# Two more 8-column products in the gate of the mLSTM branch of a hybrid layer

## The chip, the cores and the metric

The kernel runs on one core of a Trainium2 chip. The metric is the time of one execution on the device in microseconds (us), as the median over several executions. Beside it stands one execution that the hardware profiler recorded; times inside the kernel are read from that one and are counted from the start of its span.

## What is computed

One layer with two branches over 256 tokens of width 1024, all in 32-bit floats. The input is normalised and modulated by a condition vector; one wide product with `w_in` gives thirteen pieces; an attention branch and an mLSTM branch are worked out, gated, added, and multiplied by `w_out`:

```python
h = _rmsnorm(x, norm_w) * (1 + scale) + shift
(qa, ka, va, za, qm, km, vm, zm, om, ig, fg, ga, gm) = jnp.split(h @ w_in, SPLIT_IDX, axis=-1)
...
ya = (ya * jax.nn.silu(za)) @ w_att_proj
...
hm = jax.nn.sigmoid(heads(om, ML_HEADS).astype(f32)) * hm
hm = _rmsnorm(hm, ml_norm_w.reshape(ML_HEADS, 1, ML_HEAD_DIM))
ym = (merge(hm).astype(x.dtype) * jax.nn.silu(zm)) @ w_ml_proj
y = jax.nn.sigmoid(ga) * ya + jax.nn.sigmoid(gm) * ym
return x + gate * (y @ w_out)
```

The change sits in the product that gives `gm`, the gate of the mLSTM branch.

## The kernel before

Every large product is made of three products of rounded operands. A weight block is split into a high part `wh` (cast by ACT, line 472) and a low part `wl` (by DVE, line 478), the activations into `hTh` and `hTl`, and the sum high·high + high·low + low·high replaces one product at full precision.

The program is a list of chunks (`za`, `qm`, `zm`, `km`, `att`, `vm`, `ga`, `om`, `gm`, `ml`, `out` and others), each cut into steps of 256 rows of the weight matrix. The order of work is the order in which the Python code emits it, queue by queue; no scheduler moves anything. At each step the code emits the split of the block that is wanted four steps later, then the work hung on that step by `at(step, fn)` (other parts of the layer), then the step's own products.

A step of `gm` is one of the weight-stationary kind: 2 blocks of 128 rows, 4 column blocks `i` for each, and three products of 256 columns for each of these, so 24 products, every one with its own weight load. `gm` has two halves of four steps. They are called steps 1 to 8 below; step 1 starts at 270.58 us, step 2 at 275.56, step 3 at 278.39, step 4 at 282.28, step 5 at 285.11, step 6 at 288.72, step 7 at 292.43 and step 8 at 295.37.

The inner loop of such a step, with line numbers of the profile:

```python
 1205  extra = EXTRA.get((ch["name"], ch["half"], kp, i)) if kk == 0 else None
 1206  if extra == 0:
 1207      nc.tensor.matmul(aux([128, 8]), wh[:, 0, cs], sh_[:, k, 0:8], start=True, stop=True)
 1208  nc.tensor.matmul(o, wh[:, kk, cs], sh_[:, k], ...)
 1210  if extra == 1:
 1211      nc.tensor.matmul(aux([128, 8]), wh[:, 0, cs], sh_[:, k, 0:8], start=True, stop=True)
 1212  nc.tensor.matmul(o, wh[:, kk, cs], sl_[:, k], ...)
 1213  nc.tensor.matmul(o, wl[:, kk, cs], sh_[:, k], ...)
```

So a table `EXTRA` places additional products of 8 columns. Their result is never read. The key is chunk, half, step in the half and column block, counted from 0; the value 0 puts the product ahead of the first of the three, the value 1 behind it. The table before holds six of them; the one in `gm` stands in step 7.

Each additional product needs a place to write: `aux(...)` takes one of four PSUM buffers named `aux`, the one that has been released longest. The same four buffers serve the attention, the transposes and `ml_num`, and an instruction that takes a buffer waits until its last readers are done.

`ml_num(h)` is the work that stands between the steps of `gm`. For one head it takes two `aux` buffers, makes 9 products of 256 or 258 columns (lines 914 to 916), and each buffer is then read by DVE (line 918, `omt<-aux`) and by ACT (line 919, `den<-aux`). One head is emitted ahead of step 1, two heads ahead of step 2 (so all four buffers), one ahead of step 4. Ahead of steps 6 and 7 stand 8 transposes each (line 954), also into `aux`.

Of the kernel before, what the change touches and what calls it, by code (L numbers as in the profile page):

```python
# [64 lines left out]
def tile_hybrid(ctx: ExitStack, tc: tile.TileContext, x, c, params, params2, rel_t, w_row, ada_mod, ada_gate,  # L65
# [241 lines left out]

    chunks = []

    EXTRA = {('za', 0, 0, 0): 0, ('qm', 0, 2, 1): 0, ('qm', 0, 2, 2): 1, ('km', 0, 0, 0): 0, ('ga', 0, 0, 0): 0, ('gm', 1, 2, 0): 1}  # L310
    STRASSEN = ('zm', 'vm', 'om')

    def seg(kind, src, c0, name, stat=None):
# [827 lines left out]
    for g in range(NG):  # L1141
# [49 lines left out]
        for kk in range(2):  # L1191
# [9 lines left out]
            else:  # L1201
                for i in range(4):
                    cs = slice(i * 128, (i + 1) * 128)
                    o = mmt[ci][:, i]
                    extra = EXTRA.get((ch["name"], ch["half"], kp, i)) if kk == 0 else None
                    if extra == 0:
# [71 lines left out]
```

## Time and profile before

| | |
|---|---|
| median of 3 executions | 346.86 us (346.7 to 347.53) |
| the profiled execution, whole | 347.67 us |
| its span (first to last instruction) | 345.5 us |
| TensorE matmuls (PE) busy | 339.3 us, 98% of the span, 2324 instructions |
| VectorE (DVE) busy | 297.8 us, 86% |
| ScalarE (ACT) busy | 243.4 us, 70% |
| granted TensorE clock, mean | 0.999 of full |

PE is the matmul side of TensorE and PEld its weight loads, which run beside the matmuls. A busy time counts overlapping instructions once. The recorded length of one matmul (about 0.28 us for 256 columns) is longer than the distance from its start to the next one's start, since matmuls are pipelined; what a product costs is read from the distance of the starts.

### The profile page before, as it was taken

The page shows a single profiled execution, that of the slowest core. Times are in us where ns is not written, and L with a number is a line of the kernel's source. Part 1 is how long each engine was busy: PE and PEld are TensorE (multiplying, and loading weights), DVE is VectorE, ACT ScalarE, POOL GpSimd, SP SyncE. Part 2 cuts the span into 40 slices and gives each one's busy share as a digit, 9 for nine tenths or more (in the row PEclk, how much of TensorE's full clock was granted, in tenths as well). Part 3 has the DMA queues.
Part 4 walks back from the last instruction along what each step waited for, and adds up shares of the span by engine and source line. Part 5 has one row for each costly group of instructions (what it writes and reads, how often), then busy time and mean ns, then how long its engine had stood idle before and what let it go on. Part 6 is the DMA issues. An engine that isn't in the chain of part 4 may idle for free.

```text
span 345.5 us, 6083 instructions
## 1 busy us (share of the span) xinstructions
PE 339.3 (98%) x2324; PEld 315.0 (91%) x2324; DVE 297.8 (86%) x435; ACT 243.4 (70%) x376; POOL 87.8 (25%) x90
## 2 busy tenths in 40 slices
PE   8899999999999999999999999999999999999996
PEld 8778889988999999888999998899988999999885
DVE  5989996887988877999786899998988988989793
ACT  3868779989877756689688557874497758744440
POOL 4960002774100815002353273000000022500000
PEclk9999999999999999999999999999999999999999
DMA  7999999997567499179760973929969379074011
GB/s 274 413 419 417 418 390 336 258 223 308 171 224 288 64 338 282 47 296 371 262 229 2 348 201 65 379 104 335 279 184 416 112 276 409 2 262 166 2 61 61
DMA packets 30116, 83.72 MB, mean 242 GB/s; under 512 B 2176, under 2 KB 6280, under 8 KB 29576
## 3 DMA queue, kind: packets, MB, share of 16 engines
q1 hardware_dynamic: 27520, 78.08, 62.3%
q0 software_dynamic: 2112, 4.19, 7.1%
q10 hardware_dynamic: 456, 1.07, 0.9%
q8 instruction: 18, 0.29, 0.3%
q14 instruction: 10, 0.08, 0.1%
HBM read 81.89 MB, written 1.45 MB: 241 GB/s over the span
## 4 chain that ended last, share of the span: by engine, by line
PE 92%; DMA 7%; DVE 0%; ACTq 0%; issue 0%; DVEq 0%
PE mm L1208 15%; PE mm L1212 15%; PE mm L1213 15%; PE pm L192 7%; DMA adat<-in_ada_mod_dram 6%; PE aux L1187 6%; PE aux L1189 6%; PE aux L1188 6%; PE mm L1198 4%; PE mm L1200 3%; PE mm L1199 3%; PE pg L192 2%; DMA prm<-in_params_dram 1%; PE mm L1226 1%; PE mm L1225 1%; PE mm L1224 1%
## 5 line engine op out<-in xcount | busy, mean ns | idle before, releaser
L478 DVE TENSOR_TENSOR wl<-raw,wh 128x1024 fp32r<-128x1024 f32 (+2 forms) x90 | 107.0, 1214 | 16.6 <-ACT wh L472 16.6
L472 ACT CAST wh<-raw 128x1024 fp32r<-128x1024 f32 (+2 forms) x100 | 100.6, 1024 | 27.3 <-PE mm L1212 19.3
L1208 PE MATMUL mm<-hTh,wh 128*128 128x256 f32 x320 | 89.7, 280 | 0.0
L1212 PE MATMUL mm<-hTl,wh 128*128 128x256 f32 x320 | 88.8, 277 | 0.0
L1213 PE MATMUL mm<-hTh,wl 128*128 128x256 f32 x320 | 88.6, 277 | 0.0
L1213 PEld LDWEIGHTS mm<-hTh,wl 128*128 128x128 f32 x320 | 60.3, 188 | 0.0
L1208 PEld LDWEIGHTS mm<-hTh,wh 128*128 128x128 f32 x320 | 60.1, 188 | 0.1
L1212 PEld LDWEIGHTS mm<-hTl,wh 128*128 128x128 f32 x320 | 60.1, 188 | 0.0
L478 POOL TENSOR_TENSOR wl<-raw,wh 128x1024 fp32r<-128x1024 f32 x10 | 24.4, 2455 | 51.7 <-ACT wh L472 51.7
L1198 PE MATMUL mm<-wh,hTh 128*128 128x512 f32 (+2 forms) x64 | 23.0, 360 | 0.0
L1200 PE MATMUL mm<-wh,hTl 128*128 128x512 f32 (+2 forms) x64 | 22.4, 350 | 0.0
L1199 PE MATMUL mm<-wl,hTh 128*128 128x512 f32 (+2 forms) x64 | 22.4, 350 | 0.0
L181 DVE TENSOR_TENSOR wrl<-raw,wrh 128x512 fp32r<-128x512 f32 (+1 forms) x24 | 19.1, 818 | 0.3
L1187 PE MATMUL aux<-wh,Sh 128*128 128x512 f32 x48 | 18.7, 389 | 0.0
L1188 PE MATMUL aux<-wl,Sh 128*128 128x512 f32 x48 | 18.7, 389 | 0.0
L1189 PE MATMUL aux<-wh,Sl 128*128 128x512 f32 x48 | 18.7, 389 | 0.0
L151 DVE CUSTOM_DVE_ANT_0 sq<-adat,cb 128x1024 f32<-128x1024 f32 x14 | 17.1, 1218 | 1.5 <-DMA adat<-in_ada_mod_dram 1.5
L1208 PE MATMUL mm<-yah,wh 128*128 128x256 f32 x64 | 17.8, 279 | 0.0
L1213 PE MATMUL mm<-yah,wl 128*128 128x256 f32 x64 | 17.7, 276 | 0.0
L1212 PE MATMUL mm<-yal,wh 128*128 128x256 f32 x64 | 17.7, 276 | 0.0
L1213 PE MATMUL mm<-ymh,wl 128*128 128x256 f32 x64 | 17.7, 276 | 0.0
L1208 PE MATMUL mm<-ymh,wh 128*128 128x256 f32 x64 | 17.7, 276 | 0.0
(266 smaller groups left out, 842.8 us busy)
## 6 DMA issues: line engine op xcount, KB each, us to landing
raw<-in_w_in_dram SPq DMA_DIRECT2D x34, 1024.0 KB, 7.4
adat<-in_ada_mod_dram SPq DMA_DIRECT2D x16, 512.0 KB, 9.6
raw<-in_w_row_dram SPq DMA_DIRECT2D x8, 704.0 KB, 9.7
gw<-in_ada_gate_dram SPq DMA_DIRECT2D x4, 1024.0 KB, 8.9
raw<-in_w_att_proj_dram SPq DMA_DIRECT2D x4, 1024.0 KB, 9.9
raw<-in_w_ml_proj_dram SPq DMA_DIRECT2D x4, 1024.0 KB, 6.6
raw<-in_w_out_dram SPq DMA_DIRECT2D x4, 1024.0 KB, 4.9
raw<-in_w_in_dram POOLq DMA_DIRECT2D x3, 1024.0 KB, 13.1
```

Source lines behind the costliest of these rows:

```text
L192: nc.tensor.matmul(pm[ch][:, t], a[:, k, t * 128:(t + 1) * 128], b[:, cs], start=k == 0 and i == 0, stop=k == KT - 1 and i == 2)
L472: nc.scalar.copy(h, w)
L478: e.tensor_tensor(l, w, h.bitcast(F32), op=OP.subtract)
L1187: nc.tensor.matmul(o, a, wh[:, kk], start=k == 0 and p in (0, 1, 3), stop=False, skip_group_check=True)
L1188: nc.tensor.matmul(o, a, wl[:, kk], start=False, stop=False, skip_group_check=True)
L1189: nc.tensor.matmul(o, b, wh[:, kk], start=False, stop=k == 3, skip_group_check=True)
L1198: nc.tensor.matmul(o, a, wh[:, kk], start=first, stop=False)
L1199: nc.tensor.matmul(o, a, wl[:, kk], start=False, stop=False)
L1200: nc.tensor.matmul(o, b, wh[:, kk], start=False, stop=last)
L1208: nc.tensor.matmul(o, wh[:, kk, cs], sh_[:, k], start=first and i % 2 == 0, stop=False, skip_group_check=True)
L1212: nc.tensor.matmul(o, wh[:, kk, cs], sl_[:, k], start=False, stop=False, skip_group_check=True)
L1213: nc.tensor.matmul(o, wl[:, kk, cs], sh_[:, k], start=False, stop=last and i % 2 == 1, skip_group_check=True)
```

## The change

Two entries are added to the table. Nothing else differs in the code.

```diff
-    EXTRA = {('za', 0, 0, 0): 0, ('qm', 0, 2, 1): 0, ('qm', 0, 2, 2): 1, ('km', 0, 0, 0): 0, ('ga', 0, 0, 0): 0, ('gm', 1, 2, 0): 1}
+    EXTRA = {('za', 0, 0, 0): 0, ('qm', 0, 2, 1): 0, ('qm', 0, 2, 2): 1, ('km', 0, 0, 0): 0, ('ga', 0, 0, 0): 0, ('gm', 0, 1, 0): 1, ('gm', 0, 3, 0): 1, ('gm', 1, 2, 0): 1}
```

They put one 8-column product behind the first product of step 2 and one behind the first product of step 4. PE gets two more matmuls with their weight loads; the queues of DVE, ACT, POOL and SP hold the same instructions in the same order as before.

PE at the start of step 2, before. The numbers tell buffers apart: `aux_3086` is the last of the four buffers that the two heads ahead of step 2 have taken, `mm_3006` is the accumulator of `gm`.

```order
L914 MATMUL aux_3086<-vaug_2526,SD_2239 128x258
L915 MATMUL aux_3086<-vml_2527,SD_2239 128x256
L916 MATMUL aux_3086<-vaug_2526,SD_2239 128x258
L1208 MATMUL mm_3006<-hTh_71,wh_2968 128x256
L1212 MATMUL mm_3006<-hTl_72,wh_2968 128x256
L1213 MATMUL mm_3006<-hTh_71,wl_2969 128x256
```

The same place now, with the waits named (a semaphore carries the name of the engine that raises it).

```order
L914 MATMUL aux_3086<-vaug_2526,SD_2239 128x258
L915 MATMUL aux_3086<-vml_2527,SD_2239 128x256
L916 MATMUL aux_3086<-vaug_2526,SD_2239 128x258
L1208 MATMUL mm_3006<-hTh_71,wh_2968 128x256
L1211 MATMUL aux_3101<-hTh_71,wh_2968 128x8 [waits Activation_49]
L1212 MATMUL mm_3006<-hTl_72,wh_2968 128x256
L1213 MATMUL mm_3006<-hTh_71,wl_2969 128x256
```

The new product stands second in step 2 and waits for ACT. Its buffer `aux_3101` is the place in PSUM that `aux_3059` had, the first buffer of the first of the two heads, and the count it waits for is the one that ACT reaches with its read of `aux_3059`.

ACT around that read (the same rows in both programs): `den` is the read at line 919, `sqm` the square at line 921, `wh` a cast of the split.

```order
L919 ACTIVATE den_3007<-aux_3017 128x1 [waits DVE_49]
L921 ACTIVATE sqm_3026,ssq_3008<-omt_2949 128x256
L472 CAST wh_3055<-raw_2686 128x1024 [waits PE_49]
L919 ACTIVATE den_3007<-aux_3059 128x1 [waits DVE_49]
L921 ACTIVATE sqm_3065,ssq_3008<-omt_2949 128x256 [waits Activation_49]
L919 ACTIVATE den_3007<-aux_3067 128x1 [waits DVE_49]
```

The read of `aux_3059` stands behind the cast that belongs to step 2, and itself waits for DVE, whose queue holds the subtraction of that split (line 478) ahead of its own read of `aux_3059` (line 918). Nothing moved in this queue; what is new is that the product of line 1211 on PE is tied to this read.

PE at step 4, now; the product of the head ahead of it has lost its wait for ACT, since it takes the buffer of the first additional product.

```order
L914 MATMUL aux_3169<-vaug_2526,SD_2239 128x258 [waits PE_49]
L915 MATMUL aux_3169<-vml_2527,SD_2239 128x256
L916 MATMUL aux_3169<-vaug_2526,SD_2239 128x258
L914 MATMUL aux_3177<-vaug_2526,SD_2239 128x258 [waits Activation_49]
L915 MATMUL aux_3177<-vml_2527,SD_2239 128x256
L916 MATMUL aux_3177<-vaug_2526,SD_2239 128x258
L914 MATMUL aux_3177<-vaug_2526,SD_2239 128x258
L915 MATMUL aux_3177<-vml_2527,SD_2239 128x256
L916 MATMUL aux_3177<-vaug_2526,SD_2239 128x258
L1208 MATMUL mm_3006<-hTh_71,wh_2990 128x256
L1211 MATMUL aux_3204<-hTh_71,wh_2990 128x8 [waits Activation_49]
L1212 MATMUL mm_3006<-hTl_72,wh_2990 128x256
```

The wait for ACT of line 914 has moved from here to step 2. The second additional product takes the place of `aux_3078`, the first buffer of the second head ahead of step 2, and waits for ACT's read of that.

## The prediction

> **What bounds the kernel now.** I read the head of the page first, then what PE waited for, then the chain.
>
> ```profile
> span 345.5 us, 6083 instructions
> PE 339.3 (98%) x2324; PEld 315.0 (91%) x2324; DVE 297.8 (86%) x435; ACT 243.4 (70%) x376; POOL 87.8 (25%) x90
> PEclk9999999999999999999999999999999999999999
> PE 92%; DMA 7%; DVE 0%; ACTq 0%; issue 0%; DVEq 0%
> ```
>
> PE is busy for 98% of the span, and the chain that ended last lies on PE for 92% of it. The waits of PE, in full:
>
> ```profile
> PE warm L217 <- POOL ident masks.py:199: 1.4, 1, 1.4
> PE pm L192 <- DVE wrl L181: 1.0, 2, 0.6
> PE pm L192 <- ACT hTh L164: 0.5, 1, 0.5
> ```
>
> All three lines (217 and 192) belong to the opening phase. In `gm` and behind it PE waits for nobody, so a delay put into PE there has no slack to vanish in: every later product, and the output behind the last one, moves by it. For the same reason each nanosecond between two products counts. That distance has two values. The windows of two steps of 24 products with nothing else in them, step 3 of `gm` and one of `ga`:
>
> ```profile
> 278.39:281.22 2.83, 2.83 (x27) 2.83 (x25) 2.08 (x4) 2.06 (x9) 0.00 (x0) 1.00 0.91 327
> 231.40:234.12 2.72, 2.72 (x26) 2.72 (x25) 2.72 (x5) 1.06 (x1) 0.00 (x0) 1.00 0.14 15
> ```
>
> The first figure is the length of the step: 2.83 us is 118 ns a product, 2.72 us is 113 ns, both at a granted clock of 1.00. So a stretch of products runs in a wide or in a close spacing; steps 1 to 6 of `gm` run wide, and step 7, where the sixth additional product stands, goes over to close. This is read from the starts in PE's timeline. An additional product that does so in a place like the new ones, behind a first product of a wide stretch, stands in `qm`, and what followed the one in step 7 is below it:
>
> ```profile
> 125.03 0.17 PE L1207 MATMUL aux<-hTh,wh 128*128 128x8 f32 x1
> 125.06 0.36 PE L1208 MATMUL mm<-hTh,wh 128*128 128x256 f32 x1
> 125.26 0.28 PE L1212 MATMUL mm<-hTl,wh 128*128 128x256 f32 x1
> 125.38 0.28 PE L1213 MATMUL mm<-hTh,wl 128*128 128x256 f32 x1
> 125.50 0.28 PE L1208 MATMUL mm<-hTh,wh 128*128 128x256 f32 x1
> 125.62 0.17 PE L1211 MATMUL aux<-hTh,wh 128*128 128x8 f32 x1
> 125.65 0.36 PE L1212 MATMUL mm<-hTl,wh 128*128 128x256 f32 x1
> 125.85 0.28 PE L1213 MATMUL mm<-hTh,wl 128*128 128x256 f32 x1
> ...
> 292.86 0.28 PE L1213 MATMUL mm<-hTh,wl 128*128 128x256 f32 x1
> ...
> 295.37 0.28 PE L1208 MATMUL mm<-hTh,wh 128*128 128x256 f32 x1
> ```
>
> From the first product to the third it takes 0.35 us with the additional one between (125.50 to 125.85). The remaining 22 distances of step 7 take 295.37 − 292.86 = 2.51 us, which is 114 ns each: close after a few products.
>
> **The change part by part.** It removes nothing and moves nothing; it adds two products with their weight loads, and a wait.
>
> *The wait in step 2.* This is the largest term. PE and its weight loads around the place:
>
> ```profile
> 275.56 0.28 PE L1208 MATMUL mm<-hTh,wh 128*128 128x256 f32 x1
> 275.68 0.28 PE L1212 MATMUL mm<-hTl,wh 128*128 128x256 f32 x1
> 275.80 0.28 PE L1213 MATMUL mm<-hTh,wl 128*128 128x256 f32 x1
> ```
>
> ```profile
> 275.57 0.19 PEld L1212 LDWEIGHTS mm<-hTl,wh 128*128 128x128 f32 x1
> ```
>
> The new product's weight load would stand where that load stands, at 275.57. It must first see ACT's read (line 919) of the first buffer of the first head. ACT, then DVE:
>
> ```profile
> 274.91 1.04 ACT L472 CAST wh<-raw 128x1024 fp32r<-128x1024 f32 x1
> 277.57 0.17 ACT L919 ACTIVATE den<-aux 128x1 f32<-128x1 f32 x1 [1.62 <-DVE omt L918]
> ```
>
> ```profile
> 275.98 1.23 DVE L478 TENSOR_TENSOR wl<-raw,wh 128x1024 fp32r<-128x1024 f32 x1 [0.56 <-ACT wh L472]
> 277.12 1.08 DVE L918 TENSOR_TENSOR omt<-aux,omt 128x256 f32<-128x256 f32 x3
> ```
>
> The read ends at 277.57 + 0.17 = 277.74. It is late for a reason that PE can't speed up: ACT casts until 275.95, DVE subtracts until 277.2, then reads the buffer, then ACT does. What a release of PE by ACT costs is seen once in the opening phase:
>
> ```profile
> 10.86 0.60 ACT L164 ACTIVATE hTh<-xnT,Bb,Ab 128x256 fp32r<-128x256 f32 x1 [0.95 <-DVE Bb L144]
> ```
>
> ```profile
> 11.51 0.30 PEld L192 LDWEIGHTS pm<-wrh,hTh 128*128 128x128 f32 x2 [0.67 <-ACT hTh L164]
> ```
>
> ACT ends at 11.46, the load starts at 11.51: 0.05 us. So the load of the new product starts at 277.79 in place of 275.57, **2.22 us** later. Behind it on PE are queued the other 23 products of step 2 and all that follows. ACT and DVE wait for PE (buffers of `wh`) and slide with it, at most as far; their queues ahead of the read hold nothing that needs a product of step 2.
>
> *The new product itself in step 2.* First to third product takes 0.35 us with an additional one and 275.80 − 275.56 = 0.24 us without: **0.11 us**. Its 8 columns are not what it costs, since the next product is recorded only 0.03 us later (125.62 to 125.65) and the one behind that 0.20 later. The Trainium skill ("TensorE: Matmul & The Clock Gate", section "Back-to-back issue gap") has a matmul of 64 columns or fewer start its successor after some 60 cycles, with a floor of about 25 ns; by that the two new products would cost 0.05 us together in place of 0.22 and the sum below would be 0.17 lower. The 0.03 agrees with the floor, the 0.20 behind it does not fit a price of that size, and the measured 0.11 is used.
>
> *The second wait, in step 4.* It is for ACT's read of the third buffer; DVE's three reads above end at 278.20, and ACT's third follows within some 0.5 us as its first did, so it is over by 278.7, and PE comes there after 282.4. Nothing; if ACT were 3 us later, this would be the next wait.
>
> *The spacing behind the new products.* If they do what the one in `qm` did, the wide steps become close ones. The rows of the other steps:
>
> ```profile
> 282.28 0.28 PE L1208 MATMUL mm<-hTh,wh 128*128 128x256 f32 x1
> ...
> 282.51 0.28 PE L1213 MATMUL mm<-hTh,wl 128*128 128x256 f32 x1
> ...
> 285.11 0.28 PE L1208 MATMUL mm<-hTh,wh 128*128 128x256 f32 x1
> ...
> 287.93 1.03 PE L954 MATMUL aux<-ident,omt 128*128 128x128 f32 x8
> 288.72 0.36 PE L1208 MATMUL mm<-hTh,wh 128*128 128x256 f32 x1
> ...
> 291.64 0.60 PE L954 MATMUL aux<-ident,omt 128*128 128x128 f32 x4
> ```
>
> ```profile
> 90.74 0.37 PE L1208 MATMUL mm<-hTh,wh 128*128 128x256 f32 x1
> ...
> 93.56 0.38 PE L743 MATMUL aux<-kT,qT 128*128 128x256 f32 x1
> ```
>
> Step 2, the 22 distances behind its third product: 278.39 − 275.80 = 2.59 against 2.51, −0.08. Step 3: 2.83 against 2.72, −0.11. Step 4: the additional product +0.12 (0.35 against 0.23), the rest 2.60 against 2.51, −0.09; together +0.03. Step 5: 2.82 against 2.72, −0.10. Step 6 comes behind transposes; a step of `za` behind transposes that runs close takes 93.56 − 90.74 = 2.82, step 6 took 2.92: −0.10. Steps 7 and 8 run close already. Whether a close spacing comes about is bounded from both sides: none of it gives 0 for these five terms and leaves the 0.12 of step 4; all of it gives −0.48 in the steps, and up to 0.04 more if the 9 products ahead of step 4 (281.22 to 282.28) go from 118 to 113 ns too. I take the steps and leave out the 0.04, as these nine stood between no two close steps before.
>
> *Sum:* 2.22 + 0.11 − 0.08 − 0.11 + 0.03 − 0.10 − 0.10 = **+1.97 us**. Against the profiled execution that is a span of 345.5 + 1.97 = 347.5 and a whole of 347.67 + 1.97 = 349.6. That execution lies 0.8 us above the median shown; the time asked for is the median, so 346.86 + 1.97 = **348.8 us**, 0.57% longer.
>
> **The rivals.**
>
> *The wait comes, the close spacing doesn't.* The wait breaks the rhythm that the product in `qm` had around it, and shortly ahead of that one another additional product (125.03 above) left the spacing wide (125.26 to 125.38 to 125.50, 0.12 each). Then 2.22 + 0.11 + 0.12 = 2.45: 349.3. For it: no stall ahead of a stretch of 256 columns is in this trace, so the state after one is unknown.
>
> *The sixth additional product upsets what is close already.* It would now find steps 5 and 6 close, and could turn them wide from step 7 on through `ml`. That is about 23 + 24 + 192 = 239 products by 4.5 ns, 1.1 us more: 349.9. Against it: the spacing kept close behind the transposes in `za`.
>
> *PE's clock drops in the wait.* A step at half the granted clock takes 2.72 us more: 351.5 for one such step. Against it: the pause of 0.67 us quoted above and the others of PE's waits, 1.4 us in the longest, left the clock row at 9 throughout; but 2.2 us is longer than any of them. The Trainium skill (same page, "Part 1", on the clock gate) lets the clock fall after an idle window of about 3.4 us, which this wait does not reach; no run here shows it.
>
> *No wait to speak of: not slower.* If ACT's read were done before 275.52 (275.57 less the 0.05), the change would be only what its two products do: 0.11 + 0.12 − 0.48 = −0.25, 346.6, the same within what can be told. This decides at one point: how far behind 275.52 the read ends. The profile has it 2.2 us behind, held by three instructions in a row: the cast of 1.04, the subtraction of 1.23, and DVE's read from 277.12 until ACT can begin at 277.57. To fall below the 0.3% it would have to end 0.9 us earlier.
>
> **How the numbers follow.** A measurement of this kernel can tell about 0.3% from no change, 1.04 us. The forecast gets 0.62, the wait without close spacing 0.20, the upset from step 7 on 0.05, the clock 0.05, and no wait or a much shorter one 0.08. The first three and the clock are slower by over 0.3%: 0.92. Of the last 0.08, 0.06 is within 0.3% and 0.02 faster, which would need more than all the close spacing there is to win. The range runs from 348.2, 0.6 below the forecast (the spread of the three times shown is 0.8, and the 0.04), to 349.9, the third case. Outside it are the clock, the missing wait and some of the spread, under 2 in 10.
>
> **What would show it.** In the profile of the changed kernel PE, or its weight loads, should carry a wait at line 1211 for ACT's `den` of line 919, once, of some 2 us, starting near 275.6, and none for the second of these products. The starts from the product behind it on should lie some 2.3 us later than before. Steps 3 and 5 should take 2.72 us each in place of 2.83 and 2.82; if they take 2.83, the first rival holds. Steps 7 and 8 and `ml` should keep their close spacing. The clock row should stay at 9. The prediction is wrong if ACT's read comes much earlier than 277.7, or if PE does not stand still for it.

## The result, and the profile after

| | before | changed |
|---|---|---|
| median of 5 executions each, same chip | 346.86 us (346.43 to 347.62) | 349.93 us (349.28 to 351.04) |
| ratio, 95% interval | | 1.0087 (1.0072 to 1.0103) |
| the profiled execution, whole / span | 347.67 / 345.5 us | 351.04 / 348.9 us |

The change costs 3.07 us. The forecast was 1.97 us, 348.8: the sign and the cause of the larger part were right, and the time lies at the upper edge of the range (349.9), where the second rival stands.

The head of the page of the changed kernel:

```profile
span 348.9 us, 6087 instructions
PE 340.7 (98%) x2326; PEld 315.9 (91%) x2326; DVE 297.9 (85%) x435; ACT 243.0 (70%) x376; POOL 87.1 (25%) x90
PEclk9999999999999999999999999999999989999999
```

PE's busy time grew by 1.4 us and the span by 3.4, and the clock row has one 8: the 33rd of 40 slices, which begins at 279.1 us (32 × 348.9 / 40), in step 2. What the weight loads waited for (engine, tile and line, releaser, total, count, longest), and the loads around the place:

```profile
PEld aux L1211 <- ACT den L919: 2.2, 1, 2.2
```

```profile
274.83 0.19 PEld L1208 LDWEIGHTS mm<-hTh,wh 128*128 128x128 f32 x1
277.18 0.19 PEld L1211 LDWEIGHTS aux<-hTh,wh 128*128 128x128 f32 x1 [2.16 <-ACT den L919]
277.29 0.19 PEld L1212 LDWEIGHTS mm<-hTl,wh 128*128 128x128 f32 x1
```

ACT and DVE ahead of it, in the changed kernel:

```profile
276.96 0.17 ACT L919 ACTIVATE den<-aux 128x1 f32<-128x1 f32 x1 [1.63 <-DVE omt L918]
```

```profile
275.37 1.23 DVE L478 TENSOR_TENSOR wl<-raw,wh 128x1024 fp32r<-128x1024 f32 x1 [0.56 <-ACT wh L472]
276.51 1.41 DVE L918 TENSOR_TENSOR omt<-aux,omt 128x256 f32<-128x256 f32 x4
```

PE's own rows there, the first product of step 2, the new product, and the third product of the step:

```profile
274.95 0.28 PE L1208 MATMUL mm<-hTh,wh 128*128 128x256 f32 x1
277.18 0.27 PE L1211 MATMUL aux<-hTh,wh 128*128 128x8 f32 x1 [1.96 <-ACT den L919]
...
277.51 0.28 PE L1213 MATMUL mm<-hTh,wl 128*128 128x256 f32 x1
```

The wait is there once, at line 1211, for the read that was named. Step 1 starts at 269.96 here and at 270.58 before, so places are compared from the start of step 1. ACT's read ends 7.17 us behind it (276.96 + 0.17 − 269.96) and ended 7.16 behind it before; the load follows 0.05 us later (277.13 to 277.18); and it stands at 7.22 where the next load stood at 4.99 before: 2.23 us later. From the first to the third product of step 2 it takes 277.51 − 274.95 = 2.56 us against 0.24, so the wait and the new product's own slot are 2.32 together. Those two terms were forecast as 2.33.

Two more losses are not in the forecast sum. The first is in this same execution. PE's windows in the changed kernel (start:end, length, busy times of PE, PEld, DVE, ACT, POOL, granted clock, DMA): step 2 up to a point, the stretch behind it, and one step of `ml`:

```profile
274.95:278.19 3.24, 1.28 (x11) 1.08 (x10) 2.83 (x6) 1.61 (x9) 0.00 (x0) 1.00 0.98 338
278.19:281.61 3.42, 3.42 (x19) 3.42 (x17) 0.93 (x2) 0.70 (x5) 0.00 (x0) 0.50 0.70 271
...
301.44:304.16 2.72, 2.72 (x26) 2.72 (x25) 2.72 (x3) 2.25 (x3) 1.05 (x1) 1.00 0.00 0
```

```profile
277.99 0.28 PE L1208 MATMUL mm<-hTh,wh 128*128 128x256 f32 x1
278.10 0.30 PE L1212 MATMUL mm<-hTl,wh 128*128 128x256 f32 x1
278.21 0.40 PE L1213 MATMUL mm<-hTh,wl 128*128 128x256 f32 x1
278.41 0.42 PE L1208 MATMUL mm<-hTh,wh 128*128 128x256 f32 x1
278.62 0.41 PE L1212 MATMUL mm<-hTl,wh 128*128 128x256 f32 x1
```

A microsecond after PE has started again, the granted clock falls to 0.50 for 3.42 us, and the products stand 0.21 us apart in place of 0.11. Then it is full again. The step of `ml` runs close (2.72), as before.

The second loss shows itself where the clock holds. The changed kernel was run again beside other kernels, and that time the profiled execution (350.02 us, span 347.9) kept its clock. Its windows are, in this order, steps 2, 3, 4, 5, 6, 7, 8 and the first step of `ml`:

```profile
274.65:279.81 5.16, 3.20 (x27) 2.99 (x26) 3.75 (x7) 2.33 (x13) 0.00 (x0) 1.00 0.93 326
279.81:282.64 2.83, 2.83 (x26) 2.83 (x25) 1.59 (x4) 1.05 (x1) 0.00 (x0) 1.00 0.29 117
283.71:286.57 2.86, 2.86 (x28) 2.86 (x26) 2.27 (x6) 1.08 (x7) 1.30 (x2) 1.00 0.97 368
286.57:289.29 2.72, 2.72 (x26) 2.72 (x25) 2.69 (x8) 2.25 (x3) 2.06 (x3) 1.00 1.01 383
290.08:293.00 2.92, 2.92 (x27) 2.92 (x26) 2.92 (x7) 2.15 (x5) 0.00 (x0) 1.00 1.03 435
293.79:296.82 3.03, 3.03 (x29) 3.03 (x27) 1.56 (x4) 3.00 (x5) 1.88 (x1) 1.00 0.14 51
296.82:299.64 2.82, 2.82 (x26) 2.82 (x25) 2.82 (x3) 1.30 (x2) 1.94 (x2) 1.00 0.00 0
299.64:302.47 2.83, 2.83 (x26) 2.83 (x25) 2.83 (x4) 2.25 (x3) 1.05 (x1) 1.00 0.00 0
```

Step 5 is close (2.72), as forecast. Steps 3 and 6 are not. Step 8 and `ml`, which run close before (2.72 each), are wide here: 2.82 and 2.83. So the same program takes its loss in two ways, and which of them an execution shows is not the same each time.

### The profile page after: what moved, and what is told of

Same layout as the page of the kernel before. It is cut to its first block, busy times and chain, and to the rows that moved or that the text cites. A ratio compares the mean times of both kernels' runs of the same rounds, so it can differ in the third digit from the quotient of the medians.

```text
span 348.9 us, 6087 instructions
## 1 busy us (share of the span) xinstructions
PE 340.7 (98%) x2326; PEld 315.9 (91%) x2326; DVE 297.9 (85%) x435; ACT 243.0 (70%) x376; POOL 87.1 (25%) x90
## 5 line engine op out<-in xcount | busy, mean ns | idle before, releaser
L1208 PEld LDWEIGHTS mm<-hTh,wh 128*128 128x128 f32 x320 | 61.0, 191 | 0.1
L1212 PEld LDWEIGHTS mm<-hTl,wh 128*128 128x128 f32 x320 | 60.9, 190 | 0.0
```

The costliest lines, as they stand in the source:

```text
L1208: nc.tensor.matmul(o, wh[:, kk, cs], sh_[:, k], start=first and i % 2 == 0, stop=False, skip_group_check=True)
L1212: nc.tensor.matmul(o, wh[:, kk, cs], sl_[:, k], start=False, stop=False, skip_group_check=True)
```

## The experiments

The theory at the outset: the wait for ACT's read makes the loss, and the spacing of the products moves the rest. Its rivals: that the additional products cost it by themselves, through the spacing they leave behind them (above all by what happens to `ml`), and that the clock does. All kernels compute the whole layer; what is edited is where the additional products stand, where they write, or what stands ahead of the read.

The kernels ran in three groups on three chips, each group beside executions of the kernel before on the same chip: its medians there were 347.19 us (29 executions, for the first four kernels), 346.92 (20, the next four) and 347.00 (21, the last two). From one execution to the next the part ahead of `gm` takes up to a microsecond more or less (step 1 starts between 269.67 and 270.58 us in the twelve profiles), so beside the medians stands one length read from PE's timeline of each profiled execution: from the first product of step 1 of `gm` to the first product of `out` (steps 1 to 8 and all of `ml`). Before it is 319.85 − 270.58 = 49.27 us.

**The wait taken away.** Both new products stay where they are, but write into a buffer of the accumulators (`mm`, two buffers, one of them free through the first half of `gm`) in place of an `aux` buffer. Lines behind it move by one.

```diff
-    nc.tensor.matmul(aux([128, 8]), wh[:, 0, cs], sh_[:, k, 0:8], start=True, stop=True)
+    free8 = ps.tile([128, 8], F32, name="mm", bufs=2) if (ch["name"], ch["half"]) == ("gm", 0) else aux([128, 8])
+    nc.tensor.matmul(free8, wh[:, 0, cs], sh_[:, k, 0:8], start=True, stop=True)
```

> Both new products stay where they are, but write into the free accumulator of the large products in place of a buffer of ml_num, so nothing is waited for. Theory (the wait is what costs, with the drop of the clock that can follow it): no wait of PE in gm, granted clock 1.0 there, time 346.5 to 347.1 us, ratio 0.999 to 1.001. Rival (the products themselves cost, by upsetting the spacing of what follows): slower by 1 us or more, ratio above 1.003, without a wait.

Measured: 347.84 us (11 executions), ratio 1.0021 (1.0011 to 1.003). PE in it, at the new product of step 2 (now line 1212), and two steps of `ml`:

```profile
275.04 0.28 PE L1208 MATMUL mm<-hTh,wh 128*128 128x256 f32 x1
275.16 0.17 PE L1212 MATMUL mm<-hTh,wh 128*128 128x8 f32 x1
275.19 0.36 PE L1213 MATMUL mm<-hTl,wh 128*128 128x256 f32 x1
275.39 0.28 PE L1214 MATMUL mm<-hTh,wl 128*128 128x256 f32 x1
```

```profile
297.62:300.45 2.83, 2.83 (x27) 2.83 (x25) 2.83 (x4) 2.25 (x3) 1.06 (x1) 1.00 0.00 0
300.45:303.28 2.83, 2.83 (x27) 2.83 (x26) 2.83 (x5) 1.34 (x2) 0.00 (x0) 1.00 0.26 65
```

First to third product: 0.35 us, no wait. Most of the loss is gone, so the wait makes most of it; but the time misses the expected 0.999 to 1.001. What is left, about 0.7 us, is there without any wait and with the clock at 1.00: steps 2 to 5 are close and gain, but `ml` is wide. The length from step 1 to `out` is 50.18 us, 0.91 more than before.

**The product of step 2 alone**, with its wait.

```diff
-    ('gm', 0, 1, 0): 1, ('gm', 0, 3, 0): 1, ('gm', 1, 2, 0): 1}
+    ('gm', 0, 1, 0): 1, ('gm', 1, 2, 0): 1}
```

> Only the new product of step 2, with its wait. Theory: all of the loss, ratio 1.006 to 1.010, a wait of 2.2 us of the weight loads at line 1211 for ACT. Rival (each of the two products costs its share): about half, ratio near 1.004.

Measured: 349.81 us (6), ratio 1.0081 (1.0063 to 1.0098); in 2 of the 6 executions the mean clock was 0.995 (350.92 and 350.68 us), in the others it was full (349.01 to 349.90). The profiled execution is one of the latter, with the same wait of 2.2 us. Its windows: steps 2 and 3, then step 4, and a step of `ml`:

```profile
274.78:279.85 5.07, 3.10 (x27) 2.90 (x26) 3.75 (x7) 2.33 (x13) 0.00 (x0) 1.00 0.94 334
279.85:282.57 2.72, 2.72 (x26) 2.72 (x25) 1.48 (x4) 1.05 (x1) 0.00 (x0) 1.00 0.33 128
283.64:286.47 2.83, 2.83 (x26) 2.83 (x25) 2.23 (x5) 1.09 (x7) 1.30 (x2) 1.00 0.88 340
...
299.46:302.18 2.72, 2.72 (x27) 2.72 (x25) 2.72 (x3) 2.25 (x3) 1.16 (x1) 1.00 0.00 0
```

By the medians this one product brings nearly the whole loss (the profiled execution is the fastest of the six). Here steps 2 and 3 do go close behind the wait, the 9 products of `ml_num` ahead of step 4 turn it wide again, and with steps 4 to 6 wide as before, `ml` is close as before. Step 2 at a full clock is 5.07 us; in the changed kernel's first profile, with half the clock, it is 6.66 us (274.95 to 281.61). The fall of the clock costs the difference, 1.59 us (1.50 against the 5.16 us of the second profile, whose step 2 is wide behind the wait).

**The product of step 4 alone.**

```diff
-    ('gm', 0, 1, 0): 1, ('gm', 0, 3, 0): 1, ('gm', 1, 2, 0): 1}
+    ('gm', 0, 3, 0): 1, ('gm', 1, 2, 0): 1}
```

> Only the new product of step 4. Theory: no wait, so +0.12 us if the spacing stays wide behind it and -0.2 us if it turns close; ratio 0.999 to 1.001. Rival (each costs its share): ratio near 1.004.

Measured: 347.10 us (11), ratio 1.000 (0.999 to 1.0009). PE in it:

```profile
281.55 0.17 PE L1211 MATMUL aux<-hTh,wh 128*128 128x8 f32 x1
281.58 0.36 PE L1212 MATMUL mm<-hTl,wh 128*128 128x256 f32 x1
281.78 0.28 PE L1213 MATMUL mm<-hTh,wl 128*128 128x256 f32 x1
281.90 0.28 PE L1208 MATMUL mm<-hTh,wh 128*128 128x256 f32 x1
```

No wait, as forecast. But the products behind it stay 0.12 apart: this one leaves the stretch wide. It costs its slot of 0.11 us and no more. In the second profile of the changed kernel the same product made steps 4 and 5 close, in the first it did not; so the product alone does not decide it, and what does is not settled here.

**The first product moved from step 2 to step 3**, where its buffer has long been read; the product of step 4 stays.

```diff
-    ('gm', 0, 1, 0): 1, ('gm', 0, 3, 0): 1, ('gm', 1, 2, 0): 1}
+    ('gm', 0, 2, 0): 1, ('gm', 0, 3, 0): 1, ('gm', 1, 2, 0): 1}
```

> The product of step 2 stands behind the first product of step 3 instead, where ACT's read is over; that of step 4 stays; buffers as in the changed kernel. Theory: no wait of more than 0.1 us, ratio 0.999 to 1.001; if both turn the spacing close, steps 3 to 6 at 2.72 us and 0.3 us won. Rival (the products cost): ratio above 1.004.

Measured: 348.30 us (12), ratio 1.0028 (1.0019 to 1.0038), no wait at line 1211, no fall of the clock. Steps 3, 4 (behind their additional products) and 5 are close, step 6 wide; in step 7 the sixth additional product leaves a wide stretch, and `ml` takes 22.62 us in place of 21.76. The same remainder as with the wait taken away by another buffer, so it is not the buffer. The time misses the expected 0.999 to 1.001 by this remainder.

**The sixth product one column block later**, on top of the kernel without the wait. The idea was that its place against the transposes decides whether it leaves a close or a wide stretch.

```diff
-    ('gm', 1, 2, 0): 1}
+    ('gm', 1, 2, 1): 1}
```

> As e1_no_wait, but the additional product of step 7 stands behind the first product of the second column block (three products later), no longer next to the transposes. Theory (what an additional product does to the spacing hangs on the rhythm that it meets; next to these transposes it met another one than before): it may now turn steps 7, 8 and ml close, 192 products at 113 ns, so 1.0 us less than e1_no_wait, ratio 0.998 to 1.000. Rival (once the two new products are in, ml stays wide wherever the sixth stands): ratio 1.001 to 1.003, as e1_no_wait.

Measured: 347.82 us (8), ratio 1.0025 (1.0015 to 1.0034): nothing won, `ml` still wide. But PE's rows show something else:

```profile
292.25 0.28 PE L1213 MATMUL mm<-hTl,wh 128*128 128x256 f32 x1
292.37 0.28 PE L1214 MATMUL mm<-hTh,wl 128*128 128x256 f32 x1
292.49 0.28 PE L1208 MATMUL mm<-hTh,wh 128*128 128x256 f32 x1
292.60 0.17 PE L1212 MATMUL aux<-hTh,wh 128*128 128x8 f32 x1
```

Ahead of the late product the distances were shrinking by themselves (in nanoseconds 122, 116, 114), as they do where a close stretch begins; behind it they are 118. Step 7 was going close without help, and the product threw it out.

**The changed kernel again**, for a count of the executions in which the clock falls.

> The changed kernel again, for a second profile. Theory: if the granted clock holds through the wait, steps 2, 3, 5 are close, step 6 is wide behind the transposes, the sixth product fails and ml runs at 118 ns, so +2.3 from the wait and its product, -0.3 from the close steps, +1.1 from ml: some 3.1 us over before, ratio near 1.009; if the clock drops, ml stays close and the drop costs 1.7 us: some 3.9 us over. Rival (the wait is all): ml close with the clock held, 2.0 us over before.

Measured: 351.39 us (6), ratio 1.012 (1.0095 to 1.0145). The mean clock was 0.995 in 3 of the 6 (351.86, 352.64, 352.08 us) and full or 0.999 in the others (350.02, 349.67, 350.92). Its profile is the second one shown above: clock held, `ml` wide.

**A shorter wait.** Both heads that stand ahead of step 2 are emitted ahead of that step's split, so that DVE and ACT read their buffers before they subtract and cast.

```diff
-    at(s + (2 * i + 1, i)[hp], ml_num, 2 * hp + i)
+    (ahead if s + (2 * i + 1, i)[hp] == s + 1 else at)(s + (2 * i + 1, i)[hp], ml_num, 2 * hp + i)
```

> The changed kernel, with the products and reads of the two heads of step 2 emitted ahead of the split of that step, so DVE and ACT read the buffers before the subtraction and the cast. Theory: the wait falls from 2.2 to about 0.5 us, the granted clock never drops, 1.7 us less than the changed kernel, ratio to before 1.003 to 1.005 (ml wide as in e1_no_wait). Rival (the drop of the clock and the loss have another cause than the length of the wait): the ratio stays at 1.007 or above.

Measured: 347.84 us (12), ratio 1.0025 (1.0014 to 1.0036); the clock held in all 12. PE at the place:

```profile
275.41 0.28 PE L1208 MATMUL mm<-hTh,wh 128*128 128x256 f32 x1
275.86 0.27 PE L1211 MATMUL aux<-hTh,wh 128*128 128x8 f32 x1 [0.17 <-ACT den L919]
...
276.19 0.28 PE L1213 MATMUL mm<-hTh,wl 128*128 128x256 f32 x1
```

First to third product 0.78 us against 0.35 without a wait: a wait of 0.43 us is left of the 2.2, and the time falls with it to that of the kernel without one. So it is the length of the wait that counts, and ACT's read behind split and subtraction that sets it. Steps 2 to 5 are close here, and `ml` is wide.

**A longer wait.** A piece of work of DVE (`gate_acc`, 1.28 us) that stands behind the split's subtraction is emitted ahead of it in step 2.

```diff
-    for s, j in ((start("gm") + 1, 2), (start("gm") + 7, 3), (start("gm") + 7, 4), (start("ml"), 5),
+    ahead(start("gm") + 1, gate_acc, 2)
+    for s, j in ((start("gm") + 7, 3), (start("gm") + 7, 4), (start("ml"), 5),
```

> The changed kernel, with one of DVE's products for the gate vector (1.3 us) put ahead of the subtraction of step 2, so that ACT's read comes later. Theory: a wait of about 2.9 us, 0.7 us more than the changed kernel, and a granted clock below 0.997 in more of the executions than 1 in 4, since a longer pause takes more of a window. Rival (the clock falls only behind a pause of 3.4 us or more, and what was seen at 2.2 us was chance): ratio 1.010 to 1.012 and no more drops than at 2.2 us.

Measured: 353.76 us (6), ratio 1.0157 (1.0116 to 1.0198). The wait (line numbers are one higher) and the windows around it:

```profile
PEld aux L1212 <- ACT den L919: 2.7, 1, 2.7
```

```profile
274.00:277.38 3.38, 1.29 (x11) 1.08 (x9) 3.38 (x5) 1.40 (x5) 0.00 (x0) 1.00 0.86 309
277.38:284.20 6.82, 6.40 (x30) 6.40 (x31) 1.17 (x5) 2.98 (x13) 0.00 (x0) 0.50 0.47 156
284.20:287.00 2.80, 2.80 (x26) 2.80 (x26) 1.79 (x5) 0.56 (x1) 0.72 (x2) 1.00 0.28 29
```

The clock is at 0.50 for 6.82 us, twice the 3.42 of the first profile, and it falls while PE still waits. The mean clock was 0.990 in 4 of the 6 executions (353.74 to 354.21 us) and full in 2 (350.33 and 350.12). The two groups lie 3.7 us apart. Where the clock holds, half a microsecond more of wait is lost in the spread of the executions (350.33 and 350.12 against 350.02, 349.67 and 350.92 on the same chip); where it falls, the four lie some 1.8 us above the three of the changed kernel in which it fell (351.86 to 352.64).

**The sixth product left out**, on top of the kernel without the wait: if step 7 goes close by itself, `ml` should be close.

```diff
-    ('gm', 0, 1, 0): 1, ('gm', 0, 3, 0): 1, ('gm', 1, 2, 0): 1}
+    ('gm', 0, 1, 0): 1, ('gm', 0, 3, 0): 1}
```

> As e1_no_wait (both new products, nothing waited for), without the sixth additional product in step 7. Theory (in this rhythm step 7 runs close by itself behind the transposes, as its first three distances did in f1_late_sixth ahead of the product there, and the sixth product throws it out): steps 7, 8 and ml close, 0.2 to 0.4 us under before, ratio 0.9985 to 0.9997. Rival (ml stays wide in any case once the new products are in): 0.7 us over before, ratio near 1.002.

Measured: 346.57 us (11), ratio 0.9991 (0.9982 to 1.0). Its windows of steps 7 and 8 and of the first step of `ml`:

```profile
291.77:294.59 2.82, 2.82 (x28) 2.82 (x26) 1.35 (x4) 2.79 (x6) 1.66 (x1) 1.00 0.44 180
294.59:297.31 2.72, 2.72 (x27) 2.72 (x25) 2.72 (x4) 1.52 (x2) 1.84 (x2) 1.00 0.00 0
297.31:300.03 2.72, 2.72 (x27) 2.72 (x25) 2.72 (x3) 2.25 (x3) 1.37 (x1) 1.00 0.00 0
```

All close. The remainder of 0.7 us is gone, and the interval only just touches no change from below: the best version found, 0.3 to 0.4 us under the kernel before.

**The product of step 2 alone, without the wait** (the free buffer, and only that new product; the sixth stays).

```diff
-    ('gm', 0, 1, 0): 1, ('gm', 0, 3, 0): 1, ('gm', 1, 2, 0): 1}
+    ('gm', 0, 1, 0): 1, ('gm', 1, 2, 0): 1}
```

> Only the new product of step 2, written into the free accumulator, so without its wait; the sixth stays. Theory (it is a close step 5 ahead of the transposes that upsets the sixth product): steps 2 and 3 close, steps 4 to 6 wide, ml close, 0.1 us under before, ratio 0.999 to 1.0005; and 2.2 us or more under e2_step2_alone, which differs by the wait. Rival (any new product upsets the sixth): ml wide, ratio near 1.0025.

Measured: 347.05 us (11), ratio 1.0003 (0.9993 to 1.0013). Steps 2 and 3 are close, 4 to 6 wide, `ml` close. Against the same product with its wait (1.0081) this leaves 0.78% for the wait and what follows from it, 2.7 us.

All twelve traces in one table, with the length from step 1 to `out` and what stands ahead of and behind the sixth product:

| kernel | step 1 to `out`, us | against before | step 5 | `ml` |
|---|---|---|---|---|
| before | 319.85 − 270.58 = 49.27 | | wide | close |
| changed, clock fell | 323.20 − 269.96 = 53.24 | +3.97 | wide | close |
| changed again, clock held | 322.26 − 269.67 = 52.59 | +3.32 | close | wide |
| wait taken away | 320.24 − 270.06 = 50.18 | +0.91 | close | wide |
| step 2 alone | 321.22 − 269.80 = 51.42 | +2.15 | wide | close |
| step 4 alone | 319.12 − 269.73 = 49.39 | +0.12 | wide | close |
| step 3 for step 2 | 320.65 − 270.36 = 50.29 | +1.02 | close | wide |
| late sixth | 320.50 − 270.33 = 50.17 | +0.90 | close | wide |
| shorter wait | 321.04 − 270.43 = 50.61 | +1.34 | close | wide |
| longer wait, clock fell | 325.97 − 270.03 = 55.94 | +6.67 | close | wide |
| no sixth, no wait | 319.07 − 270.05 = 49.02 | −0.25 | close | close |
| step 2 alone, no wait | 319.62 − 270.41 = 49.21 | −0.06 | wide | close |

Wherever the sixth product stands in step 7 and step 5 is close, `ml` is wide (six traces); wherever step 5 is wide, `ml` is close (five). Without the sixth product `ml` is close behind a close step 5 too.

## Why the prediction was right, and where its sum was short

*The wait.* Right in place, releaser and size: 2.23 us measured, 2.22 forecast. That it makes the loss is shown by taking it away (1.0087 becomes 1.0021, for step 2 alone 1.0081 becomes 1.0003) and by changing its length.

*The new product's own slot.* Right: 0.11 us, also in step 4 alone (+0.12 over the whole length). The figure of the Trainium skill for short products would have made the pair 0.17 cheaper; the row was the better guide. The same section of the Trainium skill calls its formula that of an isolated product, which leaves out the weight load, and here every product has its own.

*The second wait, in step 4.* Right: none in any trace.

*The spacing of steps 2 to 5.* Half right. Without the wait all four go close, as forecast. Behind the wait of 2.2 us the rest of step 2 went close in two profiles (the first one of the changed kernel, until its clock fell, and step 2 alone) and stayed wide in one (the changed kernel again). The forecast of −0.08 and −0.11 for steps 2 and 3 is thus not there in each execution. Step 4's +0.03 and step 5's −0.10 came as forecast in the second profile: 2.85 against 2.83 us, and 2.73 against 2.83.

*Step 6.* Wrong: −0.10 forecast, 2.92 us before and 2.92 after, in every trace. The step of `za` behind transposes was no guide to it.

*Steps 7, 8 and `ml`.* Here the sum failed. The prediction let them keep their close spacing and gave the opposite a chance of 0.05. In the second profile of the changed kernel step 7 takes 3.02 us in place of 2.94, step 8 2.83 in place of 2.72, and `ml` 22.62 in place of 21.76 (from 299.64 to 322.26, before from 298.09 to 319.85): 0.08 + 0.11 + 0.86 = 1.05 us, near the 1.1 that the rival was priced at. Close steps 4 and 5, which the prediction counted as a gain, go with this in six traces of six, and leaving out the sixth product undoes it. The rival had named the right product. What was put against it, a spacing that stayed close behind transposes in `za`, was no test of it: no additional product follows there.

The sum of the second profile, against before: step 2 5.17 − 2.83 = 2.34; step 3 0.00; step 4 0.02; step 5 −0.10; step 6 0.00; steps 7, 8 and `ml` 1.05: together 3.31 of the 3.32 that the length grew. In the first profile it is step 2 with 6.66 − 2.83 = 3.83 and step 4, whose product left it wide, with 0.11: 3.94 of 3.97. The median grew by 3.07.

*The clock.* The rival was given 0.05 and priced as one step at half clock, 2.7 us. It happened in 6 of 17 executions behind the wait of 2.2 us (1 of 5, 2 of 6, 3 of 6), cost 1.59 us in the profile, and lasted 3.42. One ground against it was empty: the longest wait that it quoted, 1.4 us, stands at the very start of the span, and the trace's record of the clock begins only at 6.91 us. The clock row shows 9 there, but products of 128 columns start 0.21 us apart ahead of that moment and 0.11 behind it, so the clock was low already.

What decides it can be read from the traces. In all twelve each recorded change of the clock lies a whole number of times 3.413 us behind the first record (in the first profile full at 5.155 us, half at 278.222, full at 281.635). Cut into windows at these times, the traces give PE's idle time in each. The window that ended in the fall held 1.96 us of it in the first profile and 2.09 with the longer wait. Where the pause of 1.96 us left the clock full, the edge of a window cut it in two: 1.67 and 0.29 us with step 2 alone, 0.26 and 1.70 in the second profile. Over all twelve traces, the ends of the programs included, no window with 1.87 us or less was followed by a fall, and every one with 1.96 or more that was met at full clock was.

The prediction leaned on the page "TensorE: Matmul & The Clock Gate" of the Trainium skill, whose Part 1 lets the clock fall after an idle window of about 3.4 us. Its window length agrees with the 3.413 us; its condition does not, since a window idle for 1.96 us was enough. The measurement decides. The same part of the Trainium skill calls the window free-running, not tied to the program; this agrees, since the first record lies anywhere from 4.88 to 8.54 us behind the start of the span. If the edge falls anywhere with the same chance, a pause of 1.96 us lies whole in one window in (3.41 − 1.96) / 3.41 = 0.42 of the executions, an estimate; it was 6 of 17, or 0.35. No edit here moved the edge, so this rests on the traces alone.

In the profile in which the clock fell, step 5 was wide and `ml` close, so this loss came in place of the upset there and not on top of it: 1.59 there, 1.05 here. That is not a rule: with the longer wait the clock fell and `ml` was wide as well.

*The range.* The wait was forecast well; that the range holds the time is in part luck. Its upper end, 349.9, was the time of a rival with a chance of 0.05, and the median, 349.93, lies on it. The likeliest case, +1.97, is in neither profile of the changed kernel (+3.97 and +3.32). It was built from terms that fail together: when the clock holds, the close steps bring the upset; when it falls, it costs more than that. As far as two profiles can tell, the chance of 0.62 belonged to these two.

## What to carry to other kernels

A scratch product whose result nobody reads still takes a buffer in turn, and with it the wait for that buffer's last reader: before one is added, look up which buffer comes next and how far behind its reader's queue is, or give it a buffer of its own. On an engine without slack a wait of 2 us costs its length and, in a part of the executions, 1.6 us more through the clock, so it is worth removing even where it looks small. Products put in to set a rhythm depend on the rhythm that they meet: after one is added upstream, those downstream must be tried again, and here the last one is better left out.

## What the runs showed of the hardware

- The granted clock changed only at whole multiples of 3.413 us from its first record, and it fell to 0.50 at the end of such a window when PE had been idle for 1.96 us or more of it; at 1.87 us or less it never did (twelve traces).
- It came back at the end of a window in which PE had no idle time. In the first profile that was the first window behind the fall, 3.42 us; with the longer wait the first one still held 0.42 us of the pause, and the clock stayed at 0.50 for a second one, 6.82 us together.
- How often: pause of the weight loads 2.2 us, 6 of 17 executions; 2.7 us, 4 of 6; 0.43 us, 0 of 12.
- A pause can cost far more than its length: the executions in which the clock fell took 351.86 to 352.64 us with a pause of 2.2 us and 353.74 to 354.21 with one of 2.7, on the same chip.
- The same products run at 113 or at 118 ns apart for 20 us on end, and an 8-column product between them can turn either into the other. What decides which is open. In `qm` one such product left the distances at 0.12 and the next, 0.59 us later, made them 0.11; the product of step 4 left its stretch wide in two traces (alone, and in the first profile of the changed kernel) and made it close in the seven others that have it. That the outcome depends on the state that the product meets is shown by these; the rule is not.
- Behind the wait the first load comes 0.05 us after ACT's end, the next 0.11 later (277.13, 277.18, 277.29), but whether the restarted stretch is close or wide differed between two executions of the same program.
